# Even mixer of a two-block network: 8 of the 31 convolution taps as ScalarE copies added by GpSimd

## Chip, cores and metric

The kernel runs as one program on one core of a Trainium2 chip. The metric is the device time of one execution in microseconds (us); the time of the kernel before is the median of three runs. Engines are named as in the profile: PE is TensorE (PEld its weight loads), DVE is VectorE, ACT is ScalarE, POOL is GpSimd, SP is SyncE.

## What is computed

The whole network is two residual blocks of two layers each on 256 tokens of width 1024 in float32. Only one part is touched, the even mixer of the second block:

```python
def even_mixer(h, w_in, sc_conv_w, cf_conv_w, cf_conv_b, cf_ln_g, cf_ln_b, w_out):
    z = h @ w_in                                   # [256, 2560]
    sc_b, sc_c, sc_x, cf_a, cf_g = split(z)        # five parts of 512 channels
    y_sc = sc_b * causal_dwconv_2(sc_c * sc_x, sc_conv_w)       # 3 taps
    u = cf_a * jax.nn.sigmoid(cf_g)
    u = causal_dwconv_2(u, cf_conv_w) + cf_conv_b               # 31 taps
    u = jax.nn.silu(layernorm(u, cf_ln_g, cf_ln_b))
    return jnp.concatenate([y_sc, u], axis=-1) @ w_out
```

`causal_dwconv_2` is depthwise: output channel c at token t is the sum over k of w[k, c] times input channel c at token t - 30 + k.

## The kernel before

Activations stand transposed: 128 channels on the partitions, 256 tokens along the row. So the 512 channels of the convolution are four blocks of [128, 256], and the kernel works on them in two halves of two blocks (b = 0 and b = 2).

Weights come in chunks of 256 columns. `chunk` (L252) loads one into `st` by a DMA of SP and splits it in pieces of [128, 1024]: ACT rounds a piece to float32r (`whi`, L279) and DVE subtracts that from the original (`wlo`, L280). Three buffers each hold `whi` and `wlo`. A product of a piece is three matmuls per 128x128 tile (`mm3`, L285): L288 and L289 take `whi`, L290 takes `wlo`. A piece of a projection (`gather_T`) is 24 matmuls.

`even` (L1236) does this. `glu` makes `u` for two blocks from the chunks pa and pg, with 30 columns of zeros ahead of the tokens. The 31 taps are shared out. Taps 0 to 11 are `conv_pe` (L1269): ACT writes a diagonal matrix `dg` with the tap's weights (L1277), and PE multiplies it by the shifted `u` (L1278) and adds up in the PSUM tile `pcv`. Tap 30 with the bias is one ACT instruction per block that begins `cv` (L1288). Taps 12 to 29 are `conv_dve`: one DVE instruction per tap and block, cv = u * weight + cv (L1292). L1298 then adds `pcv` to `cv`. `short` (L1300) makes the gated three-tap convolution from the chunks pc, px and pb: t = pc * R * R, cx = px * t, three taps into `cs` (ACT L1312, DVE L1314), a GpSimd product cs * R (L1316), y = pb * cs (L1319), and its split into `yh`, `yl`. `norm` (L1325) needs all four blocks of `cv`: the mean over channels by ones on PE (`pmean`, L1329), the difference (L1332), squares on ACT, their sum on PE (`pvar`, L1340), a chain of small DVE instructions for 1/sqrt, its spread over the partitions (`prow`, `RL`), scale, tanh, and `yh`, `yl` of blocks 4 to 7 (L298, L299).

The output product `pr` has two passes of four chunks: the first over blocks 0 to 3 (the short convolution), the second over blocks 4 to 7 (the normed long one). The second pass ends in the residual and begins the next feed-forward.

Steps of these parts are woven when the program is written (L1364 to L1366), and then the tile framework's scheduler, which plays the program through with its own estimates, sets the order on each engine. Each engine runs its own queue strictly in that order and waits on semaphores where it needs another's result.

Of the kernel before, what the change touches and what calls it, by code (L numbers as in the profile page):

```python
# [27 lines left out]
def _runs(*spans):  # L28
    """Chunks of 256 columns of the spans."""
    return [[(c, c + 256)] for a, b in spans for c in range(a, b, 256)]  # L30
# [10 lines left out]
def _rows(chunks, *kts):  # L41
    """Each chunk's columns with the row tiles (first, count) cut after kts."""
    cuts = [(sum(kts[:i]), k) for i, k in enumerate(kts)]
    return [(c, cut) for c in chunks for cut in cuts]


# Each weight's chunks: their columns, and their row tiles of 128 as (first, count).
# [22 lines left out]
def _pack(w, chunks):  # L70
    """[L, K, N] as the chunks one after the other, each [128, row tiles, columns]."""
    layers, n = w.shape[0], w.shape[-1]
    w = w.reshape(layers, -1, 128, n)
    parts = []
    for l in range(layers):
        for pieces, (k0, kk) in chunks:
            v = np.concatenate([w[l, k0:k0 + kk, :, a:b] for a, b in pieces], axis=2)
            parts.append(v.transpose(1, 0, 2).reshape(-1))
    return np.concatenate(parts)


def _lay_out_params(inp):
    """The small parameters side by side as [128, n]: channels on partitions, or copied to all."""
    cols = []

    def chan(a):
        a = np.asarray(a).reshape(-1, 128)
        cols.append(a.T)

    def taps(a):  # L90
        k, c = a.shape
        cols.append(a.reshape(k, c // 128, 128).transpose(2, 1, 0).reshape(128, -1))

    def row(a):
        cols.append(np.broadcast_to(np.asarray(a).reshape(1, -1), (128, np.asarray(a).size)))

    def pad(a):
        c = np.zeros((128, 1), np.float32)
        c[:a.size, 0] = a
        cols.append(c)  # L100

    at = {}

    def put(name, f, a):
        at[name] = sum(c.shape[1] for c in cols)
        f(a)

    put("ffa_norm0", chan, inp["ffa_norm"][0])
    put("first", chan, inp["ffa_norm"][1])
    at["ffa_norm1"] = at["first"]  # L110
    for l in range(2):
        for nm in ("mix_norm", "ffb_norm", "mla_cq_norm", "mla_ckv_norm"):
            put(f"{nm}{l}", chan, inp[nm][l])
        for nm in ("mla_q_norm", "mla_k_norm"):
            put(f"{nm}{l}", pad, inp[nm][l])
            put(f"{nm}_rope{l}", row, inp[nm][l][64:96])
        for nm in ("moba_q_norm", "moba_k_norm", "gdn_a_log", "gdn_dt_bias"):
            put(f"{nm}{l}", row, inp[nm][l])
        put(f"gdn_conv{l}", taps, inp["gdn_conv"][l])
        put(f"gdn_out_norm{l}", chan, inp["gdn_out_norm"][l])  # L120
        put(f"mix2_norm{l}", chan, inp["mix_norm_g_2"][l])
        put(f"ffn_norm{l}", chan, inp["ffn_norm_g_2"][l])
        put(f"ffn_conv_w{l}", taps, inp["ffn_conv_w_2"][l])
        put(f"ffn_conv_b{l}", chan, inp["ffn_conv_b_2"][l])
    put("sc_conv", taps, inp["ev_sc_conv_w_2"][0])
    put("cf_conv", taps, inp["ev_cf_conv_w_2"][0])
    put("cf_b", chan, inp["ev_cf_conv_b_2"])
    put("ln_g", chan, inp["ev_cf_ln_g_2"])
    put("ln_b", chan, inp["ev_cf_ln_b_2"])
    put("lru_conv", taps, inp["od_lru_conv_w_2"][0])  # L130
    put("lru_conv_b", chan, inp["od_lru_conv_b_2"])
    put("lru_ba", chan, inp["od_lru_ba_2"])
    put("lru_bx", chan, inp["od_lru_bx_2"])
    put("lru_lam", chan, inp["od_lru_lam_2"])
    for nm in ("od_q_norm_g_2", "od_k_norm_g_2"):
        put(nm, chan, np.concatenate([inp[nm][0], inp[nm][0]]))
    return at, np.concatenate(cols, axis=1)


def _constants():  # L140
    """Tables that depend on shapes alone, side by side as [128, n]."""
# [34 lines left out]
def _all(gen):  # L176
    """Emits the rest of a part; returns what it returns."""
    while True:
        try:
            next(gen)  # L180
        except StopIteration as e:
            return e.value


def _mix(main, fill, ratio):
    """Emits a part with ratio steps of another after each of its own."""
    due = 0.0
    while True:
        try:
            next(main)  # L190
        except StopIteration as e:
            return e.value
        due += ratio
        while due >= 1:
            due -= 1
            next(fill, None)


def _weave(*gens):
    """Steps of several parts in turn."""  # L200
# [11 lines left out]
def _chain(*gens):  # L212
    """One part after the other; those not begun or not finished stay usable."""
# [5 lines left out]
class _Net:  # L219
# [32 lines left out]
    def chunk(self, name, i, between=None):  # L252
        """Chunk i of a weight, split exactly into two float32r parts: its pieces, each (first row
        tile, row tiles, high part, low part)."""
# [30 lines left out]
    def mm3(self, out, a, b, start, stop, **kw):  # L285
        """lhsT.T @ rhs of two split operands."""
# [14 lines left out]
    def rsqrt(self, v, n, name="rs"):  # L301
        """1/sqrt of a small tile of positive values."""
# [12 lines left out]
    def softplus(self, dst, x, n):  # L315
        """max(x, 0) + log1p(exp(-|x|)), the logarithm as 2 atanh(u / (2 + u))."""
# [16 lines left out]
    def rows(self, cols, name):  # L333
        """[128 tokens, 2] per-token values as a row over all partitions, [128, 256]."""
# [33 lines left out]
    def stats(self):  # L368
        """1/rms of the residual, per token as columns and as a row."""
# [15 lines left out]
    def gather_T(self, p, xs, pieces, first, last, col=0, blocks=2):  # L385
        """Adds the pieces' products to [128 features, blocks, 256 tokens] in one bank, in steps."""
# [8 lines left out]
    def gather_nat(self, p, xs, pieces, first, last, cols):  # L395
        """The same as [128 tokens, 2, cols]."""
# [21 lines left out]
    def residual(self, gain, name, layer, kts, xs, scale=None):  # L418
        """x += (a product in blocks of 128 features) [* R * scale], with the next norm's parts on
        the way; without a next norm, x goes out."""  # L420
# [130 lines left out]
    def heads(self, big, at, qk, v, sc, nsc):  # L551
        """Eight heads; qk(j) makes the transposed q and k of heads 2 j and 2 j + 1."""
# [27 lines left out]
    def rope(self, at, x, heads, d, tabs, t):  # L580
        """x [128, heads, d] in place; tabs hold gain * cos and gain * (sin, -sin)."""
# [106 lines left out]
    def gates(self, l, big, out, n, c):  # L688
        """Adds to out the tanh of half the branch's gate logits in half c of the channels."""
# [9 lines left out]
    def merge(self, l, big, mg, n, gate, br, last=None):  # L699
        """mg += 2 sigmoid(gate) * (branch @ w_branch)."""  # L700
# [191 lines left out]
    def gdn_gates(self, l, gp, csb):  # L892
        """beta and the decays: of each token from its chunk's start and to its end, of each chunk."""
# [32 lines left out]
    def gdn_decay(self, gp, scal):  # L926
        """[token, (tile, head), token of the chunk]: beta * decay, and the transposed decay."""
# [19 lines left out]
    def gdn_conv(self, l, big, wk, i):  # L947
        """2 silu(conv(.)) of the queries, keys or values, [128 dims, head, token]."""
# [20 lines left out]
    def gdn_keys(self, gk, at, raw, Dn):  # L969
        """The normalised keys and A, the strictly lower products that are to be inverted."""  # L970
# [40 lines left out]
    def inner(self, p, a, b):  # L1011
        """a.T @ b of each head's chunks, from [128 dims, (head, token)]."""
# [6 lines left out]
    def gdn_rest(self, out, wk, raw, scal, Dt, kn, knT):  # L1019
        """What the recurrence needs of the queries, the values and the keys."""  # L1020
# [46 lines left out]
    def gdn_invert(self, wk, A):  # L1067
        """Transposed inverses of I + A, by doubling the size of the inverted blocks."""
# [54 lines left out]
    def gdn_solve(self, out, us, M):  # L1123
        """u = (I + A)^-1 (v beta), and w = (I + A)^-1 (k beta exp(gcum)) transposed."""
# [19 lines left out]
    def gdn_scan(self, big, wk, scal, out, us, sz):  # L1144
        """The recurrence over the chunks, and the gated norm of what it gives."""
# [90 lines left out]
    def even(self, gain):  # L1236
        nc = self.nc
        v2 = lambda a: a.rearrange("p (b s) -> p b s", b=2)
        taps, on_pe = 31, 12
        with ExitStack() as ctx:  # L1240
# [12 lines left out]
            def glu(c):  # L1253
                """2 a sigmoid(g) of half c of the channels."""
# [14 lines left out]
            def conv_pe(b):  # L1269
                """Some of the taps of blocks b and b + 1 as products with diagonal matrices."""  # L1270
# [12 lines left out]

            def conv_dve(b):
# [5 lines left out]
                for k in range(on_pe, taps - 1):  # L1290
# [7 lines left out]
                nc.vector.tensor_tensor(cv[:, b:b + 2, :], cv[:, b:b + 2, :], v2(pcv[b]), op=OP.add)  # L1298

            def short(c):  # L1300
                """The gated short convolution of half c of the channels."""
# [23 lines left out]
            def norm():  # L1325
                """silu of the layer norm of the convolution."""
# [37 lines left out]
            fill = _chain(_weave(*(_chain(conv(0), conv(2)) for conv in (conv_pe, conv_dve))), norm())  # L1364
# [13 lines left out]
    def odd(self, gain):  # L1378
        nc = self.nc
        v2 = lambda a: a.rearrange("p (b s) -> p b s", b=2)  # L1380
        with ExitStack() as ctx:
# [43 lines left out]
            def qkv(i, z):  # L1425
                """The queries, keys or values; the first two normalised and transposed."""
# [135 lines left out]
    def lru_core(self, big, wk, xc, wa, wx, hs):  # L1562
        """The gated linear recurrence over the tokens."""
# [114 lines left out]
```

## Time and profile before

| | |
|---|---|
| time of three runs | 2027.24 us median, 2027.05 to 2028.5 |
| span of the profiled execution | 2022.9 us |
| PE busy over the span | 1997.5 us (99%) |
| DVE, ACT, POOL busy | 1450.4 us (72%), 1032.8 us (51%), 127.1 us (6%) |
| even mixer, from its first projection to its last | about 1402 to 1515 us after the start |

The span runs from the first to the last instruction of one execution; the device time of a run contains about 4.3 us more. Shares of the whole span are averages over stages with different limits, so the stage of the even mixer has to be read by itself. A busy PE is pipelined: a matmul of [128, 256] in float32r lasts 0.28 us in the record, but the next one starts 0.12 us after it, so a duration is not a price; the distance between two starts is. The same holds, less strongly, for DVE.

### The profile page before, as it was taken

Reading aid. Unit: us, or ns where it says so; the run is one execution under the profiler, and the core shown is the slowest. Engines: PE = TensorE matmul, PEld = TensorE weight load, DVE = VectorE, ACT = ScalarE, POOL = GpSimd, SP = SyncE. Lnnn points to the kernel's source line nnn. Section 1 sums busy time; section 2 is a strip of 40 time slices with the busy share of each in tenths; the row PEclk is TensorE's granted clock in tenths of the full one; section 3 lists DMA queues with packets and bytes.
Section 4 is the critical chain, followed back from the end, with each engine's and each line's share of the span. In section 5 each row is a group of like instructions: output and inputs, shape, how many; then the busy total and the mean of one; then the engine's idle time right before and its main releaser. Section 6 shows DMA issues by size and latency. Waiting matters only on the chain.

```text
span 2022.9 us, 40575 instructions
## 1 busy us (share of the span) xinstructions
PE 1997.5 (99%) x17004; PEld 1944.5 (96%) x17004; DVE 1450.4 (72%) x2585; ACT 1032.8 (51%) x1556; POOL 127.1 (6%) x158
## 2 busy tenths in 40 slices
PE   8999999999999999999999999999999999999999
PEld 8999998889999999999998999999999999989999
DVE  6665898747766676668987586666988866968874
ACT  5444665434544444446654454444655544656552
POOL 0000030220000000001203100000000000020000
PEclk9999999999999999999999999999999999999999
DMA  6455443224555555555432255555345555416554
GB/s 253 177 176 184 172 159 126 94 83 147 188 183 175 185 188 187 176 176 176 140 128 82 84 176 179 188 175 184 121 146 187 176 184 201 157 53 213 184 177 136
DMA packets 50711, 327.53 MB, mean 162 GB/s; under 512 B 6624, under 2 KB 8672, under 8 KB 18528
## 3 DMA queue, kind: packets, MB, share of 16 engines
q1 hardware_dynamic: 49296, 324.09, 45.8%
q8 instruction: 133, 2.18, 0.4%
q10 hardware_dynamic: 1232, 0.85, 0.2%
q14 instruction: 50, 0.41, 0.1%
HBM read 323.87 MB, written 1.05 MB: 161 GB/s over the span
## 4 chain that ended last, share of the span: by engine, by line
PE 95%; DVE 3%; issue 1%; ACT 1%; DMA 0%; POOL 0%; SPq 0%; DVEq 0%; ACTq 0%; POOLq 0%
PE pr L288 7%; PE pr L289 7%; PE pr L290 7%; PE pg L290 6%; PE pg L288 6%; PE pg L289 6%; PE pu L290 6%; PE pu L288 6%; PE pu L289 6%; PE pga L288 2%; PE pga L289 2%; PE pga L290 2%; PE pb L288 1%; PE pb L289 1%; PE pb L290 1%; PE pmq L288 1%
## 5 line engine op out<-in xcount | busy, mean ns | idle before, releaser
L279 ACT ACTIVATE whi<-st 128x1024 fp32r<-128x1024 f32 (+2 forms) x628 | 651.2, 1038 | 828.6 <-PE pr L289 201.6
L280 DVE TENSOR_TENSOR wlo<-st,whi 128x1024 fp32r<-128x1024 f32 (+2 forms) x628 | 756.9, 1206 | 383.7 <-ACT whi L279 378.7
L288 PE MATMUL pg<-xh,whi 128*128 128x256 f32 x1088 | 309.5, 284 | 9.3 <-ACT whi L279 9.3
L290 PE MATMUL pg<-xh,wlo 128*128 128x256 f32 x1088 | 309.1, 284 | 1.0 <-DVE wlo L280 1.0
L289 PE MATMUL pg<-xl,whi 128*128 128x256 f32 x1088 | 308.8, 284 | 0.0
L290 PE MATMUL pu<-xh,wlo 128*128 128x256 f32 x1056 | 299.6, 284 | 0.2 <-DVE wlo L280 0.2
L288 PE MATMUL pu<-xh,whi 128*128 128x256 f32 x1056 | 299.3, 283 | 0.0
L289 PE MATMUL pu<-xl,whi 128*128 128x256 f32 x1056 | 299.1, 283 | 0.0
L290 PE MATMUL pr<-gh,wlo 128*128 128x256 f32 x1056 | 297.4, 282 | 0.0
L289 PE MATMUL pr<-gl,whi 128*128 128x256 f32 x1056 | 297.4, 282 | 0.0
L288 PE MATMUL pr<-gh,whi 128*128 128x256 f32 x1056 | 297.4, 282 | 0.0
L288 PEld LDWEIGHTS pg<-xh,whi 128*128 128x128 f32 x1088 | 209.7, 193 | 9.3 <-ACT whi L279 9.3
L290 PEld LDWEIGHTS pg<-xh,wlo 128*128 128x128 f32 x1088 | 209.6, 193 | 1.5 <-DVE wlo L280 1.5
L289 PEld LDWEIGHTS pg<-xl,whi 128*128 128x128 f32 x1088 | 209.7, 193 | 0.0
L290 PEld LDWEIGHTS pu<-xh,wlo 128*128 128x128 f32 x1056 | 202.8, 192 | 0.4 <-DVE wlo L280 0.4
L288 PEld LDWEIGHTS pu<-xh,whi 128*128 128x128 f32 x1056 | 202.9, 192 | 0.0
L289 PEld LDWEIGHTS pu<-xl,whi 128*128 128x128 f32 x1056 | 202.9, 192 | 0.0
L288 PEld LDWEIGHTS pr<-gh,whi 128*128 128x128 f32 x1056 | 199.0, 188 | 0.0
L289 PEld LDWEIGHTS pr<-gl,whi 128*128 128x128 f32 x1056 | 199.0, 188 | 0.0
L290 PEld LDWEIGHTS pr<-gh,wlo 128*128 128x128 f32 x1056 | 198.9, 188 | 0.0
L288 PE MATMUL pga<-xh,whi 128*128 128x256 f32 x384 | 112.5, 293 | 0.0
L289 PE MATMUL pga<-xl,whi 128*128 128x256 f32 x384 | 109.3, 285 | 0.0
(548 smaller groups left out, 4029.6 us busy)
## 6 DMA issues: line engine op xcount, KB each, us to landing
st<-in_w_in_dram SPq DMA_DIRECT2D x52, 1024.0 KB, 4.8
st<-in_ffb_w_in_dram SPq DMA_DIRECT2D x44, 1024.0 KB, 4.9
st<-in_ffa_w_in_dram SPq DMA_DIRECT2D x43, 1024.0 KB, 4.8
st<-in_ffn_w_gate_dram SPq DMA_DIRECT2D x22, 1024.0 KB, 4.9
st<-in_ffn_w_up_dram SPq DMA_DIRECT2D x22, 1024.0 KB, 4.9
st<-in_ffa_w_out_dram SPq DMA_DIRECT2D x16, 896.0 KB, 4.5
st<-in_ffb_w_out_dram SPq DMA_DIRECT2D x16, 896.0 KB, 4.5
st<-in_ffn_w_down_dram SPq DMA_DIRECT2D x16, 896.0 KB, 4.5
```

Source lines behind the costliest of these rows:

```text
L279: self.hi = nc.scalar.activation(hi[:, :m], s, AF.Copy).ins
L280: nc.vector.tensor_tensor(lo[:, :m], s, hi[:, :m].bitcast(F32), op=OP.subtract)
L288: mm(out, a[0], b[0], start=start, stop=False, **kw)
L289: mm(out, a[0], b[1], start=False, stop=False, **kw)
L290: mm(out, a[1], b[0], start=False, stop=stop, **kw)
```

## The change

Docstrings and comments are gone, which moves line numbers by up to 15 and does nothing else. The core:

```diff
-        taps, on_pe = 31, 12
+        taps, on_pe, on_pool = 31, 6, 14
...
+            cp = big.tile([128, 4, S], F32, name="cp")
+
+            def conv_pool(b):
+
+                while b not in have:
+                    yield
+                for k in range(on_pe, on_pool):
+                    t = cp[:, b:b + 2, :] if k == on_pe else wk.tile([128, 2, S], F32, tag="ct", bufs=3, name="ct")
+                    for e in range(2):
+                        nc.scalar.activation(t[:, e, :], u[:, b + e, k:k + S], AF.Copy, scale=CW(b + e, k))
+                    if k > on_pe:
+                        nc.gpsimd.tensor_tensor(cp[:, b:b + 2, :], cp[:, b:b + 2, :], t, op=OP.add)
+                    yield
...
-                for k in range(on_pe, taps - 1):
+                for k in range(on_pool, taps - 1):
...
                 nc.vector.tensor_tensor(cv[:, b:b + 2, :], cv[:, b:b + 2, :], v2(pcv[b]), op=OP.add)
+                nc.vector.tensor_tensor(cv[:, b:b + 2, :], cv[:, b:b + 2, :], cp[:, b:b + 2, :], op=OP.add)
...
-            fill = _chain(_weave(*(_chain(conv(0), conv(2)) for conv in (conv_pe, conv_dve))), norm())
+            fill = _chain(_weave(*(_chain(conv(0), conv(2)) for conv in (conv_pe, conv_pool, conv_dve))), norm())
```

Taps 0 to 5 stay on PE, taps 14 to 29 on DVE. Taps 6 to 13 are new: for each tap and half ACT writes u * weight into `ct` (three buffers; the first tap straight into `cp`), and GpSimd adds `ct` to `cp`. At the end DVE adds `cp` to `cv`. Per half that is 16 ACT copies, 7 GpSimd adds of [128, 512] and one DVE add.

The scheduler's order moves with it. On GpSimd the adds come ahead of the two products cs * R of the short convolution (13 of 14 ahead of the first):

```order
-L1411 MEMSET lz 128x2x3 x2
 L1246 MEMSET u 128x4x30
-L1304 MEMSET cx 128x2x2 x2
-L1316 TENSOR_TENSOR cs<-cs,R 128x512 x2
+L1319 MEMSET cx 128x2x2 x2
+L1295 TENSOR_TENSOR cp<-cp,ct 128x512 x13
+L1331 TENSOR_TENSOR cs<-cs,R 128x512
+L1295 TENSOR_TENSOR cp<-cp,ct 128x512
+L1331 TENSOR_TENSOR cs<-cs,R 128x512
+L495 MEMSET z 128x2x2 x2
```

So where that queue held two products in this stage, it now holds sixteen operations of the same size. On DVE, the end of the convolution; first the kernel before, from the last long row of taps to the difference from the mean:

```order
L1292 SCALAR_TENSOR_TENSOR cv<-u,cw,cv 128x256 x9
L280 TENSOR_TENSOR wlo<-st,whi 128x1024
L1292 SCALAR_TENSOR_TENSOR cv<-u,cw,cv 128x256
L1298 TENSOR_TENSOR cv<-cv,pcv 128x512
L1292 SCALAR_TENSOR_TENSOR cv<-u,cw,cv 128x256 x3
L1308 TENSOR_TENSOR cx<-px,t_17690 128x2x256
L1292 SCALAR_TENSOR_TENSOR cv<-u,cw,cv 128x256
L280 TENSOR_TENSOR wlo<-st,whi 128x1024
L1298 TENSOR_TENSOR cv<-cv,pcv 128x512
L1314 SCALAR_TENSOR_TENSOR cs<-cx,P,cs 128x256 x4
L280 TENSOR_TENSOR wlo<-st,whi 128x1024
L1332 TENSOR_TENSOR cv<-cv,mean 128x1024
```

And the same place of the changed kernel:

```order
L1329 SCALAR_TENSOR_TENSOR cs<-cx,P,cs 128x256 x2
L1306 SCALAR_TENSOR_TENSOR cv<-u,cw,cv 128x256 x2
L280 TENSOR_TENSOR wlo<-st,whi 128x1024
L1329 SCALAR_TENSOR_TENSOR cs<-cx,P,cs 128x256 x2
L1306 SCALAR_TENSOR_TENSOR cv<-u,cw,cv 128x256 x5
L1334 TENSOR_TENSOR y<-pb,cs 128x512
L1306 SCALAR_TENSOR_TENSOR cv<-u,cw,cv 128x256 x3
L296 TENSOR_TENSOR yl<-y,yh 128x512
L1306 SCALAR_TENSOR_TENSOR cv<-u,cw,cv 128x256
L1312 TENSOR_TENSOR cv<-cv,pcv 128x512
L1313 TENSOR_TENSOR cv<-cv,cp 128x512
L280 TENSOR_TENSOR wlo<-st,whi 128x1024
```

The second half of the short convolution (cs, y, yl) stood behind the end of the long one and now stands ahead of it. On PE the second `pmean`, which waits for that end, stood among the matmuls of the chunk pb:

```order
L289 MATMUL pb<-xl,whi 128x256
L1329 MATMUL pmean<-cv,ones 128x256 x2
L290 MATMUL pb<-xh,wlo 128x256
L288 MATMUL pb<-xh,whi 128x256
L289 MATMUL pb<-xl,whi 128x256
```

In the changed kernel the same instruction stands in the first pass of the output product:

```order
L289 MATMUL pr<-yl,whi 128x256
L1344 MATMUL pmean<-cv,ones 128x256 x2
L290 MATMUL pr<-yh,wlo 128x256
L288 MATMUL pr<-yh,whi 128x256
L289 MATMUL pr<-yl,whi 128x256
```

Ahead of it 48 matmuls of that pass have to be done, and 46 more stand between it and `pvar`. In the odd mixer behind, a few matmuls of one attention head change places; nothing is added or taken away there.

## Rows read from the trace of the kernel before

**Rows 1.** Page, part 1: busy us, share of span, instructions.

```profile
PE 1997.5 (99%) x17004; PEld 1944.5 (96%) x17004; DVE 1450.4 (72%) x2585; ACT 1032.8 (51%) x1556; POOL 127.1 (6%) x158
```

**Rows 2.** Windows: length, busy PE, PEld, DVE, ACT, POOL, PEclk, DMA share, GB/s.

```profile
1428.50:1477.70 49.20, 49.20 (x335) 46.55 (x335) 47.64 (x96) 29.49 (x61) 3.04 (x1) 1.00 0.27 92
1477.70:1498.40 20.70, 18.73 (x154) 18.21 (x152) 17.36 (x36) 10.07 (x13) 1.30 (x1) 1.00 0.44 133
```

**Rows 3.** Tile pcv (durations ns, first and last start), and one step of the chain.

```profile
L1278 PE MATMUL pcv<-u,dg x96: 376/379/382, 1429.7 to 1474.5; 128*128 128x256 f32 x96
...
1437.88 0.43 PE pcv L1278 x2
```

**Rows 4.** Groups by line, 1428.5 to 1477.7: busy us, mean ns, idle before.

```profile
L1277 ACT ACTIVATE dg<-C,cw 128x128 f32<-128x128 f32 x44 | 17.2, 398 | 14.0 <-PE pcv L1278 13.5
...
L1312 ACT ACTIVATE cs<-cx,P 128x256 f32<-128x256 f32 x4 | 1.8, 498 | 0.2 <-DVE cx L1308 0.2
...
L1292 DVE SCALAR_TENSOR_TENSOR cv<-u,cw,cv 128x256 f32<-128x256 f32 x72 | 29.9, 471 | 0.0
L280 DVE TENSOR_TENSOR wlo<-st,whi 128x1024 fp32r<-128x1024 f32 x11 | 13.9, 1265 | 0.5 <-ACT whi L279 0.4
```

**Rows 5.** Timeline of DVE in the middle of the convolution: start, duration.

```profile
1444.19 0.67 DVE L1308 TENSOR_TENSOR cx<-px,t 128x512 f32<-128x512 f32 x1
1444.79 0.46 DVE L1292 SCALAR_TENSOR_TENSOR cv<-u,cw,cv 128x256 f32<-128x256 f32 x1
1445.18 1.21 DVE L280 TENSOR_TENSOR wlo<-st,whi 128x1024 fp32r<-128x1024 f32 x1
1446.32 1.66 DVE L1292 SCALAR_TENSOR_TENSOR cv<-u,cw,cv 128x256 f32<-128x256 f32 x4
```

**Rows 6.** Timeline of DVE and POOL around the first product cs * R.

```profile
1452.20 2.06 DVE L1292 SCALAR_TENSOR_TENSOR cv<-u,cw,cv 128x256 f32<-128x256 f32 x5
1452.36 3.04 POOL L1316 TENSOR_TENSOR cs<-cs,R 128x512 f32<-128x512 f32 x1 [47.74 <-DVE cs L1314]
1454.68 1.80 DVE L280 TENSOR_TENSOR wlo<-st,whi 128x1024 fp32r<-128x1024 f32 x1 [0.42 <-ACT whi L279]
```

**Rows 7.** Timelines of two other places where POOL and DVE overlap.

```profile
1479.48 1.30 POOL L1316 TENSOR_TENSOR cs<-cs,R 128x512 f32<-128x512 f32 x1 [24.07 <-DVE cs L1314]
1479.70 2.16 DVE L280 TENSOR_TENSOR wlo<-st,whi 128x1024 fp32r<-128x1024 f32 x1 [0.30 <-ACT whi L279]
...
276.67 1.53 POOL L586 TENSOR_TENSOR work<-mq,tqbcos 128x512 f32<-128x512 f32 x1 [19.43 <-DVE gy L962]
...
276.95 1.53 DVE L962 SCALAR_TENSOR_TENSOR gy<-gz,P,gy 128x256 f32<-128x256 f32 x1
```

**Rows 8.** Timelines from the convolution's end to the second output pass.

```profile
1477.14 0.68 DVE L1298 TENSOR_TENSOR cv<-cv,pcv 128x512 f32<-128x512 f32 x1
...
1480.56 1.03 PE L1329 MATMUL pmean<-cv,ones 128*128 128x256 f32 x4
...
1484.45 1.95 PE L1340 MATMUL pvar<-ones,sq 128*128 128x1 f32 x16 [0.36 <-ACT sq L1335]
...
1486.44 0.16 DVE L1343 TENSOR_SCALAR vln<-pvar 128x2 f32<-128x2 f32 x1 [0.79 <-PE pvar L1340]
...
1491.59 0.42 DVE L341 COPY RL<-prow 128x256 f32<-128x256 f32 x1
...
1498.38 0.62 PE L288 MATMUL pr<-yh,whi 128*128 128x256 f32 x3 [1.60 <-ACT yh L298]
...
1499.89 0.38 PE L289 MATMUL pr<-yl,whi 128*128 128x256 f32 x1 [0.89 <-DVE yl L299]
```

**Rows 9.** Timeline of PE at the program's start.

```profile
9.31 0.58 PE L288 MATMUL pg<-xh,whi 128*128 128x256 f32 x1 [9.31 <-ACT whi L279]
...
11.17 0.41 PE L289 MATMUL pg<-xl,whi 128*128 128x256 f32 x1
...
13.43 0.28 PE L288 MATMUL pg<-xh,whi 128*128 128x256 f32 x1
```

## The prediction

> **What bounds the kernel now.** I read the page's busy shares first. TensorE is busy 99% of the span [rows 1], which says that any matmul taken away shortens the program, but that is an average over 2023 us. So I read the stage next, in the view by windows [rows 2]. From 1428.5, where VectorE begins the taps, to 1477.7, where the convolution is closed, TensorE is busy 49.2 of 49.2 us and VectorE 47.6 of 49.2. Both are full; the reader is to see that the second number matters as much as the first. In the next window, from there to the first matmul of the second output pass, TensorE has lost 2 of 20.7 us: it waits for the layer norm's result, 1.60 us for `yh` and 0.89 us for `yl` [rows 8]. So the stage ends when VectorE's chain ends, and TensorE's matmuls only fill the time up to it. ScalarE has 29.5 of 49.2 us and GpSimd 3.0.
>
> **TensorE, taken away.** Each diagonal product is two records, one step of 0.43 us in the chain of work [rows 3]; 96 records are 48 products. 24 go: 24 x 0.43 = 10.3 us of TensorE's work between 1429 and 1475. This is the whole gain that can be had, and it counts only if VectorE comes free earlier too.
>
> **VectorE, the queue up to the close of the convolution.** Call the end of the last addition to `cv` the close. Prices are distances between starts [rows 5]: a tap 0.39 to 0.40 us (four in 1.66 us, the last 0.47 long), a weight split 1.14 (1445.18 to 1446.32), an operation of [128, 512] 0.60 (1444.19 to 1444.79). Before: 72 taps x 0.397 = 28.6 [rows 4], 10 splits x 1.14 = 11.4, 4 taps of `cs` 1.6, 9 operations of [128, 512] 5.4, together 47.0, and about 2 us of waits and of a stretched split; the close is at 1477.14 + 0.59 = 1477.7 [rows 8]. After: the order puts ahead of the close 64 taps (25.4), 13 splits (14.8), all 8 taps of `cs` (3.2), and 13 operations of [128, 512] (7.8), since `y`, `yl` and the two additions of `cp` now stand there: 51.2 us. ScalarE makes the first two copies ahead of `cv`'s start (two of 0.4 to 0.5 us, of which some 0.3 us are not covered), which delays the first tap. With no wait at all the close is at 1428.5 + 0.3 + 51.2 = 1480.0, **2.3 us later** than before. The 8 taps saved (3.2 us) are outweighed by work that the new order moved ahead.
>
> **GpSimd's adds, the disputed price.** 14 adds of [128, 512] are new, and both products cs * R now stand ahead of the close: 16 operations. One lasts 1.30 us where nothing held it up [rows 7], so GpSimd itself has room: 16 x 1.30 = 21 of 50 us. But the trace shows that the two engines take turns. At 1452.36 a GpSimd product begins while VectorE runs five taps; it takes 3.04 us and ends at 1455.40, which is 1.1 us after the last of the five taps, and the split that VectorE began at 1454.68 takes 1.80 instead of 1.21 [rows 6]. At 1479.48 the GpSimd product keeps its 1.30, and VectorE's split takes 2.16, 0.95 more [rows 7]. At 276.67 a GpSimd product waits for the end of one tap of another convolution, and the next tap, of the same form as ours, takes 1.53 instead of 0.47: 1.06 more [rows 4, 7]. In each case one engine stood still until the other had finished its instruction. The Trainium skill, page "SBUF — State Buffer", section "SBUF: two separate sides", states this as a rule that speaks against the change: a port pair that both engines use is locked for a whole instruction, by a GpSimd operation or by a VectorE one with two SBUF inputs, and the other blocks. By that rule alone the sum would take 16 x 1.30 = 20.8 us where the row of the tap gives 17.0; the trace agrees with it in kind.
>
> Taps, splits and `cs` have two inputs in SBUF; they are 43 of the 51 us. VectorE's queue there is full, so what stops it is not made up. Bounds: the smallest loss of the three rows, 0.59, gives 16 x 0.59 = 9.4 us; the whole length, 1.30, gives 20.8. I take the row that is nearest, a tap in a full queue: 16 x 1.06 = 17.0, and take off a tenth, an assumption, since `t`, `cx`, `y` and the additions of `pcv` read one input from PSUM (8 x 0.6 = 4.8 of 51 us) and may not compete: **15.3 us**. It does not matter who wins a turn: all 16 have to be done before the close, because VectorE waits there for `cp`, and `y` waits for cs * R behind the adds. The close is then at 1480.0 + 15.3 = 1495.3.
>
> **ScalarE.** 24 diagonals go (24 x 0.40 = 9.6 us) and 32 copies come (32 x 0.50 = 16 us; both [rows 4]): 29.5 + 6.4 = 36 us in a stretch that is now 66 long, so it hides. Queued behind the copies are the splits `whi`; a copy waits for one of three `ct` buffers, that is for the add three places ahead. The adds are ahead of that as long as GpSimd gets its turns, so I take 0, with up to 3 us in the range.
>
> **From the close to the second output pass.** Before, L289 of that pass starts at 1499.89, 22.2 us after the close [rows 8]. After, TensorE's order decides. `yl` of the short convolution ends 0.4 + 0.6 + 0.6 = 1.6 us ahead of the close (one tap, two additions). Then come 42 of the 48 matmuls ahead of the second `pmean`, at 0.12 each 5.0 (154 records in 18.73 us, [rows 2]), and 0.87 for the first `pmean`: the second starts 4.3 us after the close. It takes 0.87, and 46 more matmuls 5.5: `pvar` is at close + 10.7; its squares, 3.9 us after `pmean` as before (1480.56 to 1484.45), are there by 8.2. From `pvar` to `vln` 2.0, to `RL` 5.15 with one split in between as before, and from `RL` to L289 8.3 less the three splits that stand there no more, 8.3 - 3 x 1.14 = 4.9 [rows 8]. Sum 10.7 + 2.0 + 5.15 + 4.9 = 22.8, **0.6 us more** than before. So what TensorE saves ends as waiting: ahead of the first output pass and ahead of the second, each some 8 to 10 us.
>
> **TensorE's clock.** After standing idle for 9.31 us at the start, its matmuls last 0.41 us until about 13.3 and 0.28 from 13.43 on [rows 9]: some 4 us at half pace, which costs 2 us. The 1.60 us of idle time before 1498.38 were followed by no such stretch. The two new waits are as long as the first case: 0 to 2 x 2 us. The Trainium skill, "TensorE: Matmul & The Clock Gate", section "What's actually happening", says that the gate halves the clock of an array that stood idle; by it the upper end would hold. I take **2 us**, halfway, since the granted clock reads 1.00 (the upper level, 2.4 GHz) in both windows of [rows 2], with idle time in the second, and the start may be a case of its own.
>
> **Sum.** 2.3 + 15.3 + 0.6 + 2 = 20.2 us. On the profiled execution that is a span of 2022.9 + 20.2 = 2043; on the median 2027.24 + 20.2 = **2047 us**, 1% slower. Range of this case: 2027.2 + 2.3 + 9.4 + 0.6 = 2039.5 to 2027.2 + 2.3 + 20.8 + 0.6 + 4 + 3 = 2058. A measurement of this kernel can tell 0.2%, about 4 us, from no change.
>
> **Rivals.**
> *Adds covered.* The adds fall beside work that doesn't compete, or in gaps. For it: VectorE has gaps when it waits for `whi`, and one operation in ten reads PSUM. Against it: 97% busy before (47.6 of 49.2), and the three rows above. Price: L near 0 to 4 us, so 2027.2 + 2.3 + 0.6 + (0 to 4) = 2030 to 2034; taken as 2030.
> *TensorE decides, and the change is faster.* Place: the first output pass. If VectorE's queue reached the close early enough, the stage would shrink by the matmuls: 2027.2 - 10.3 = 2017. The second pass would then have to start at 1499.9 - 10.3 = 1489.6, so the close, 22.8 us ahead of that, at 1466.8: VectorE would have to do its 51.2 us of instructions in 38. For it stands only TensorE's 99%. Even a gain of 4 us needs 44.5.
> *ScalarE blocks the splits.* If the adds starve behind taps that follow one another (four taps passed GpSimd's product at 1452), copies wait for `ct`, and the `whi` behind them too, and TensorE and VectorE wait for those. The waits would come on top: with one tap row of nine (3.6 us) lost at each of three such places, 2047 + 11 = 2058, and more.
> *The change doesn't do what it says.* The order shows 24 products, 64 taps, 14 adds and 32 copies, so only the scheduler's shifts in the odd mixer are left, and they add no work: nearly excluded.
>
> **How the numbers follow.** Turns, as summed: 0.74. Adds covered: 0.11. TensorE decides: 0.04. ScalarE blocks: 0.10. Nothing of it: 0.01. The range leaves out the covered case (0.11), the faster ones (0.05) and the far end of the blocked one; from 2036, a little under the lower bound for a few adds in gaps, to 2058. Faster by over 0.2%: 0.05. Within 0.2%: most of the covered case, 0.08. Slower: 0.87.
>
> **What would show it.** In the profile after, taps (L1306) with a mean above 0.47 us, some of 1.4 to 1.6, and splits of 1.8 to 2.3 between 1428 and 1496; GpSimd adds that begin where the last ended and last 1.3 to 2.5; the difference from the mean some 20 us later than 1482; TensorE with idle time in front of `pr`, released by `yl` and `yh`, 10.3 us and more than the 2.5 before. Wrong: taps that stay at 0.47 while adds run (then the turns fall, and the time is near 2030), `whi` on ScalarE waiting for GpSimd (then the blocked case), or a close before 1480.

## The result: 0.85% slower, 2045.4 us where 2047 was predicted

| | before | after |
|---|---|---|
| median, us | 2027.83 (2027.05 to 2028.5, 4 runs) | 2045.36 (2044.58 to 2045.69, 4 runs) |
| span of the profiled execution, us | 2022.9 | 2043.8 |

The ratio is 1.0085, 95% interval 1.0073 to 1.0097: 17.5 us more by the medians, 20.9 by the two profiled spans. The working below accounts for the spans. In every execution with both figures on record the device time is 1.8 us above the span (2045.64 against 2043.8), not 4.3 as reckoned ahead of the prediction, so the profiled execution of the kernel before took about 2024.7 us, 3 less than its median (its runs beside the experiments go from 2024.8 to 2032.3), and that is the gap between the two figures.

The page of the changed kernel, part 1 (busy us, share of the span, instructions), answers to [rows 1].

```profile
PE 1998.2 (98%) x16956; PEld 1944.4 (95%) x16956; DVE 1463.3 (72%) x2579; ACT 1036.0 (51%) x1564; POOL 151.2 (7%) x172
```

TensorE has 48 matmul records fewer and is busy 0.7 us longer; GpSimd is busy 24 us longer for 14 instructions. The stage is seen in the view by windows, which answers to [rows 2] (length, busy PE, PEld, DVE, ACT, POOL with counts, granted clock, DMA share, GB/s): from the first tap to the close of the convolution, from there to the second output pass, and two stretches of TensorE at half pace.

```profile
1429.00:1496.04 67.04, 52.43 (x347) 48.84 (x346) 65.81 (x98) 35.36 (x72) 28.64 (x16) 0.90 0.28 91
1496.04:1517.50 21.46, 13.53 (x94) 12.93 (x93) 12.53 (x29) 7.55 (x10) 0.00 (x0) 0.74 0.45 147
...
1493.20:1499.80 6.60, 6.47 (x31) 6.17 (x32) 3.36 (x7) 1.06 (x1) 0.00 (x0) 0.55 0.00 0
...
1517.40:1523.10 5.70, 5.65 (x26) 5.64 (x27) 1.34 (x2) 0.63 (x1) 0.21 (x4) 0.50 0.00 0
```

The first window was 49.2 us long and is 67.0. VectorE fills it as before (65.8), TensorE no longer does (52.4 of 67.0), and GpSimd's busy time went from 3.0 to 28.6 us. What fills VectorE is in the groups by line (busy us, mean ns of one, idle time before them and who ended it), against [rows 4].

```profile
L1306 DVE SCALAR_TENSOR_TENSOR cv<-u,cw,cv 128x256 f32<-128x256 f32 x64 | 40.6, 683 | 0.0
L1295 POOL TENSOR_TENSOR cp<-cp,ct 128x512 f32<-128x512 f32 x14 | 22.7, 1619 | 35.0 <-ACT ct L1293 34.6
...
L1293 ACT ACTIVATE ct<-u,cw 128x256 f32<-128x256 f32 x28 | 12.2, 493 | 0.0
...
L1331 POOL TENSOR_TENSOR cs<-cs,R 128x512 f32<-128x512 f32 x2 | 6.0, 3006 | 23.0 <-DVE cs L1329 23.0
```

72 taps had a mean of 471 ns; 64 have 683. The change took 8 taps from VectorE, and yet the taps keep it busy 10.7 us longer (40.6 against 29.9). Where the time sits is plain in VectorE's timeline (start, duration), to be held against [rows 5] and [rows 6].

```profile
1429.02 6.75 DVE L1306 SCALAR_TENSOR_TENSOR cv<-u,cw,cv 128x256 f32<-128x256 f32 x9
1435.69 1.78 DVE L1264 SCALAR_TENSOR_TENSOR u<-z,ua 128x512 f32<-128x512 f32 x1
...
1452.76 2.06 DVE L1306 SCALAR_TENSOR_TENSOR cv<-u,cw,cv 128x256 f32<-128x256 f32 x5
...
1455.88 4.37 DVE L1306 SCALAR_TENSOR_TENSOR cv<-u,cw,cv 128x256 f32<-128x256 f32 x3
...
1491.82 0.69 DVE L1334 TENSOR_TENSOR y<-pb,cs 128x512 f32<-128x512 f32 x1 [1.16 <-POOL cs L1331]
...
1495.44 0.69 DVE L1313 TENSOR_TENSOR cv<-cv,cp 128x512 f32<-128x512 f32 x1
```

The last of these rows is the close, at 1495.44 + 0.60 = 1496.04.

And GpSimd's timeline of the same stretch:

```profile
1430.23 4.46 POOL L1295 TENSOR_TENSOR cp<-cp,ct 128x512 f32<-128x512 f32 x3 [25.09 <-ACT ct L1293]
1435.34 1.58 POOL L1295 TENSOR_TENSOR cp<-cp,ct 128x512 f32<-128x512 f32 x1 [0.65 <-ACT ct L1293]
...
1442.37 1.28 POOL L1295 TENSOR_TENSOR cp<-cp,ct 128x512 f32<-128x512 f32 x1 [0.22 <-ACT ct L1293]
...
1454.14 7.23 POOL L1295 TENSOR_TENSOR cp<-cp,ct 128x512 f32<-128x512 f32 x4 [5.30 <-ACT ct L1293]
```

Nine taps beside three adds take 6.75 us; without adds they take 3.64 (eight steps of 0.397 and a last one of 0.47, [rows 4, 5]). The difference is 3.11, three times 1.04. Five taps at 1452.76 take 2.06, which is undisturbed, though GpSimd's row of four begins at 1454.14; its first add let the last of them and the split behind them pass. Three taps at 1455.88, beside that group of four adds, take 4.37 instead of 1.26: again 3.11. The fourth stall of the group is the tap of `cs` behind them, 1.48 instead of 0.47.

### The profile page after: what moved, and what is told of

It reads as the page before. It is cut to its first block, busy times and chain, and to the rows that moved or that the text cites. A ratio compares the mean times of both kernels' runs of the same rounds, so it can differ in the third digit from the quotient of the medians.

```text
span 2043.8 us, 40507 instructions
## 1 busy us (share of the span) xinstructions
PE 1998.2 (98%) x16956; PEld 1944.4 (95%) x16956; DVE 1463.3 (72%) x2579; ACT 1036.0 (51%) x1564; POOL 151.2 (7%) x172
## 3 DMA queue, kind: packets, MB, share of 16 engines
HBM read 323.87 MB, written 1.05 MB: 159 GB/s over the span
## 4 chain that ended last, share of the span: by engine, by line
PE 92%; DVE 5%; issue 1%; ACT 1%; DMA 1%; POOL 0%; DVEq 0%; SPq 0%; ACTq 0%; POOLq 0%
PE pr L288 7%; PE pr L289 7%; PE pr L290 7%; PE pg L290 6%; PE pg L288 6%; PE pg L289 6%; PE pu L290 6%; PE pu L288 6%; PE pu L289 6%; PE pga L288 2%; PE pga L289 2%; PE pga L290 2%; DVE cv L1306 2%; DVE wlo L280 1%; PE pb L288 1%; PE pb L289 1%
## 5 line engine op out<-in xcount | busy, mean ns | idle before, releaser
L289 PE MATMUL pg<-xl,whi 128*128 128x256 f32 x1088 | 308.6, 284 | 0.0
L289 PE MATMUL pu<-xl,whi 128*128 128x256 f32 x1056 | 298.8, 283 | 0.0
L289 PE MATMUL pr<-gl,whi 128*128 128x256 f32 x1056 | 297.2, 281 | 0.0
L289 PEld LDWEIGHTS pg<-xl,whi 128*128 128x128 f32 x1088 | 209.7, 193 | 0.0
L289 PEld LDWEIGHTS pu<-xl,whi 128*128 128x128 f32 x1056 | 202.7, 192 | 0.0
L289 PEld LDWEIGHTS pr<-gl,whi 128*128 128x128 f32 x1056 | 198.8, 188 | 0.0
L289 PE MATMUL pga<-xl,whi 128*128 128x256 f32 x384 | 109.2, 284 | 0.0
```

The costliest lines, as they stand in the source:

```text
L289: mm(out, a[0], b[1], start=False, stop=False, **kw)
```

## The experiments

All times are medians; each ratio is to the kernel before on the same chip. The close is the end of the last addition to `cv`, as in the prediction. The theory was that VectorE's queue sets the close, that each GpSimd operation beside it stops it for about 1.04 us, and that TensorE's work is worth nothing while this holds. The rival was that TensorE's order, or the weaving of the code, makes the loss. The stage itself begins 0.5 to 1.4 us later in these profiled executions than in that of the kernel before, so distances within the stage say more than absolute times.

### Only TensorE's half of the change

```diff
-                    for k in range(on_pe):
+                    for k in range(6):
```

> The kernel before with 6 of the 12 diagonal products left out and nothing in their place (24 products, 10.3 us of TensorE; so part of the convolution is missing). Theory (VectorE's queue bounds the stage, TensorE only fills it): the order puts 72 taps, 12 splits, 8 taps of cs and 11 operations of [128, 512] ahead of the convolution's close, 28.6 + 13.7 + 3.2 + 6.6 = 52.1 us where 49.2 were, so no gain: 2028 to 2033 us. Rival (TensorE bounds the stage, what it is spared comes off): 2017 us.

Measured: 2031.04 us, ratio 1.0025 (1.0012 to 1.0037). 24 products, 10.3 us of TensorE's work, are gone, nothing takes their place, and the kernel is not faster. VectorE's timeline:

```profile
1480.07 0.69 DVE L1319 TENSOR_TENSOR y<-pb,cs 128x512 f32<-128x512 f32 x1 [0.57 <-POOL cs L1316]
...
1482.97 0.69 DVE L1298 TENSOR_TENSOR cv<-cv,pcv 128x512 f32<-128x512 f32 x1
```

TensorE's:

```profile
1479.55 2.07 PE L1329 MATMUL pmean<-cv,ones 128*128 128x256 f32 x4 [3.42 <-DVE cv L1298]
...
1504.00 1.01 PE L288 MATMUL pr<-yh,whi 128*128 128x256 f32 x3 [4.54 <-ACT yh L298]
```

The close moved from 1477.73 to 1483.6, later, not earlier; from the first tap it is 53.8 us away where it was 49.2. VectorE's taps are all there (72), but in the new order all 8 taps of `cs`, two more splits, `y` and `yl` stand ahead of the close: 52.0 us of instructions at the prices of the prediction instead of 47.0. TensorE spends what it saved waiting, 3.4 us for `cv`, 3.2 ahead of `prow` and 4.5 for `yh`. So this run has the queue's term without GpSimd's: with TensorE's shorter work the program's order hands VectorE the short convolution earlier.

### Only GpSimd's adds, and half of them

```diff
+            def idle_adds(b):
+                while b not in have:
+                    yield
+                for k in range(7):
+                    nc.gpsimd.tensor_tensor(sp, sp, u[:, b:b + 2, k:k + S], op=OP.add)
+                    yield
```

> The kernel before, all taps where they were, with 14 GpSimd adds of [128, 512] of shifted u into a scratch tile that nothing reads; VectorE's order stays that of the kernel before. Theory (a GpSimd add and a VectorE instruction with two SBUF inputs take turns, 1.04 us lost per add): VectorE's queue grows by 14 x 1.04 = 14.6 us, some of it in its 1.5 us of gaps: 2039 to 2044 us, with taps of about 1.5 us in the trace. Rival (the new order, the copies or the missing products made the changed kernel slow, the adds are covered): 2028 us.

> The kernel before, with 7 of the 14 idle GpSimd adds of the earlier run (4 while the first two channel blocks are at work, 3 in the second two). Theory: each add costs VectorE's queue one turn, so half the adds cost about half: the close 5 to 7 us later than before (14 adds: 11.8 us) and 2031 to 2036 us, part of it covered by slack behind the close. Rival: the first adds alone upset the balance, or it is GpSimd's being busy at all that slows VectorE; then the loss is near that of 14, 2038 to 2042, or near none.

With the second kernel only k = 0, 2, 4, 6 of the first two blocks and 1, 3, 5 of the others are added. VectorE's instructions up to the close are those of the kernel before, one by one. Measured: 14 adds 2041.4 us, ratio 1.0073 (1.0056 to 1.009); 7 adds 2034.93 us, 1.0038 (1.0023 to 1.0053). The taps in the groups by line, with 14 adds:

```profile
L1302 DVE SCALAR_TENSOR_TENSOR cv<-u,cw,cv 128x256 f32<-128x256 f32 x72 | 40.6, 618 | 0.0
```

With 7 adds:

```profile
L1302 DVE SCALAR_TENSOR_TENSOR cv<-u,cw,cv 128x256 f32<-128x256 f32 x72 | 34.7, 538 | 0.0
```

The close, with 7 adds and then with 14:

```profile
1483.19 0.68 DVE L1308 TENSOR_TENSOR cv<-cv,pcv 128x512 f32<-128x512 f32 x1
...
1489.57 0.67 DVE L1308 TENSOR_TENSOR cv<-cv,pcv 128x512 f32<-128x512 f32 x1
```

That is 1483.8 and 1490.2, where it was 1477.73 with no added work. Part of this is the later start: counted from the second instruction of L1262 ahead of the taps (1424.42, 1425.43 and 1425.86 in the three kernels), the close comes 5.1 and 11.0 us later. The rows of VectorE that are longer than unstalled add up to 6.4 and 12.3 us, so an add costs 0.9 us however many there are; 1.3 us of either sum were covered by waits that VectorE had before. The adds' results are read by nobody, so this is not data that somebody waits for. One row of VectorE's timeline with 14 adds shows the price at its clearest:

```profile
1439.66 6.75 DVE L1302 SCALAR_TENSOR_TENSOR cv<-u,cw,cv 128x256 f32<-128x256 f32 x5
```

Five taps that take 2.06 us alone take 6.75 here: 4.69 more, 0.94 for each of the five adds between them. Why it is 0.9 here and 1.04 in the changed kernel is open. The kernels lose more than their closes, 7.5 and 13.3 us by the medians. With 7 adds TensorE runs at half pace in the second output pass (granted clock 0.61 from 1505.8 to 1514.5), with 14 at a place far behind the mixer (0.57 from 1804 to 1816), so the price is read from the rows and not from these times.

### One input instead of two

The same fourteen instructions as copies, `nc.gpsimd.tensor_copy(sp, u[:, b:b + 2, k:k + S])`.

> The kernel before, with 14 GpSimd copies of [128, 512] (one input in SBUF, where an add has two) beside the taps, into a tile that nobody reads; VectorE's own order is as before. Theory: any GpSimd instruction on SBUF takes its turn with VectorE's taps, so the copies stop them as the adds did, by something between half an add's price (one input of two, 0.5 us) and the whole (1.04 us): 14 x 0.5 to 14 x 1.04 = 7 to 14.5 us on the close, 2033 to 2041 us, and taps with a mean well over 0.47. Rival: only an operation with two inputs in SBUF competes; taps stay at 0.47 and the time at 2027 to 2029.

Measured: 2030.16 us, ratio 1.0013 (1.0003 to 1.0022), under both bounds of the theory and a little over the rival's. The groups:

```profile
L1302 DVE SCALAR_TENSOR_TENSOR cv<-u,cw,cv 128x256 f32<-128x256 f32 x72 | 34.6, 535 | 0.0
...
L1291 POOL COPY sp<-u 128x512 f32<-128x512 f32 x14 | 11.4, 812 | 23.1 <-DVE u L1264 22.3
```

The taps took 4.7 us more (29.9 before), so copies compete as well. Of these, 1.0 is the price of the product cs * R, which fell on a split before, and `u` and two splits were held up beside the copies for another 0.9; all the rows that lengthened beside copies give 4.5 us, 0.32 for each, about a third of an idle add. The close came at 1481.6, 3.9 us later, 3.2 of them after the later start of the stage. The kernel lost 2.8. Why a copy costs a third and not a half is open.

### The change with adds of 8 columns

```diff
-                        nc.gpsimd.tensor_tensor(cp[:, b:b + 2, :], cp[:, b:b + 2, :], t, op=OP.add)
+                        nc.gpsimd.tensor_tensor(cp[:, b:b + 2, 0:8], cp[:, b:b + 2, 0:8], t[:, :, 0:8], op=OP.add)
```

> The changed kernel with the 14 GpSimd adds on 8 of the 256 columns only (the rest of the 8 taps is left out); copies, buffers and waits stay. Theory (the adds' length is the price): the close comes at 1428.8 + 25.4 + 13.7 + 3.2 + 7.8 = 1479, plus 1 to 3 us for two full products and 14 short adds: 2029 to 2034 us. Rival (ScalarE's copies, their three buffers and the order are the price): 2041 us or more.

Measured: 2026.76 us, ratio 0.9997 (0.9987 to 1.0006), 2 us under what was expected. ScalarE's 32 copies and the missing products are all there, and ahead of the close stand the same instructions, a few taps and splits in other places; only the adds' length is gone, and with it the loss: 1.0085 less 0.9997 is 17.8 us. So the change gains nothing even with adds that cost almost nothing. Its taps and adds, its first taps and its close:

```profile
L1306 DVE SCALAR_TENSOR_TENSOR cv<-u,cw,cv 128x256 f32<-128x256 f32 x64 | 29.1, 506 | 0.0
L1295 POOL TENSOR_TENSOR cp<-cp,ct 128x16 f32<-128x16 f32 x14 | 8.7, 623 | 39.5 <-ACT ct L1293 39.4
...
1429.44 3.64 DVE L1306 SCALAR_TENSOR_TENSOR cv<-u,cw,cv 128x256 f32<-128x256 f32 x9
...
1481.13 0.69 DVE L1313 TENSOR_TENSOR cv<-cv,cp 128x512 f32<-128x512 f32 x1
```

The close at 1481.7 is where it was expected; the 2 us lie behind it, where the second output pass begins 18.6 us after the close (21.4 in the changed kernel).

### The change with the adds on VectorE

The same line as `nc.vector.tensor_tensor` over all columns.

> The changed kernel with the 14 adds on VectorE instead of GpSimd (0.60 us each, 8.4 us in the full queue). Theory (an add on GpSimd costs VectorE 1.04 us, more than doing it itself): faster than the changed kernel by 14 x 0.44 = 6 us less what the order changes: 2037 to 2042 us. Rival (the adds on GpSimd cost VectorE little and another wait is the price): 8 us slower than the changed kernel, about 2054 us.

Measured: 2036.34 us, ratio 1.0046 (1.0031 to 1.0061), 0.7 us under the range that was expected.

```profile
L1306 DVE SCALAR_TENSOR_TENSOR cv<-u,cw,cv 128x256 f32<-128x256 f32 x64 | 27.5, 471 | 0.0
L1295 DVE TENSOR_TENSOR cp<-cp,ct 128x512 f32<-128x512 f32 x14 | 10.0, 711 | 0.0
...
1429.52 1.66 DVE L1306 SCALAR_TENSOR_TENSOR cv<-u,cw,cv 128x256 f32<-128x256 f32 x4
...
1489.27 0.69 DVE L1313 TENSOR_TENSOR cv<-cv,cp 128x512 f32<-128x512 f32 x1
```

The taps are back at 471 ns. VectorE does the fourteen adds itself in 10.0 us and the kernel is about 8 us faster than with GpSimd's help (1.0085 less 1.0046). ScalarE's copies, which both have, do not explain the loss. This gives the price once more without any list of stalls: from the first tap to the close are 52.3 us with adds of 8 columns, 60.4 with the adds on VectorE and 67.0 with the adds on GpSimd. That is 0.58 us for an add that VectorE makes itself and 1.05 for one that GpSimd makes.

### What TensorE and VectorE are worth, apart and together

VectorE's side is cut by `for k in range(18, taps - 1)` in place of `range(on_pe, taps - 1)`; the second kernel has that and the cut of the first experiment.

> The kernel before, with 6 of VectorE's 18 taps of each channel block left out and nothing in their place (the taps' share of the convolution is missing): 24 instructions x 0.397 = 9.5 us less on VectorE; TensorE keeps all 48 products. Theory: TensorE was full as well up to the close (49.2 of 49.2 us in the kernel before), so only its 2.5 us of waiting ahead of the second output pass can be had: 2025 to 2028 us. The close of the convolution comes near 1467 (the order puts 35.7 us of instructions ahead of it, with 2 us of waits), and that gains nothing by itself. Rival, VectorE alone is the bound: 2028 - 9.5 = 2018.

> The kernel before, with 6 of TensorE's 12 diagonal products and 6 of VectorE's 18 taps of each channel block left out, nothing in their place (half of TensorE's and a third of VectorE's part of the convolution is missing): 10.3 us less on TensorE and 9.5 us less on VectorE. Theory: the two engines were balanced, and only both cuts together shorten the stage: about 10 us, 2016 to 2021 us, where the cut on TensorE alone gave +0.25% and the cut on VectorE alone should give at most 2.5. Rival, something else sets the end of the stage (ScalarE's splits, the weights' transfers): within 4 us of the kernel before, 2024 to 2030.

Measured: 2026.29 us, ratio 0.9996 (0.9987 to 1.0006) with VectorE's cut; 2017.9 us, ratio 0.9953 (0.994 to 0.9967) with both. This gives a square: 10.3 us off TensorE alone +0.25%, 9.5 us off VectorE alone nothing, both together -9.5 us by the ratio. With VectorE's cut alone it is VectorE that waits, as the view by waits (waiter and tile, who ended it: us, times, longest) shows:

```profile
DVE t L1306 <- PE pc L290: 3.2, 1, 3.2
DVE cv L1298 <- PE pcv L1278: 2.5, 1, 2.5
```

So the close did not come near 1467, as expected, but at 1477.0, held by TensorE's products (1476.42, the end of the second wait) much where it stood before. The stage was balanced: either engine alone holds the close. The 2.5 us of waits ahead of the second output pass stayed (1.60 for `yh` and 0.95 for `yl`, much as in [rows 8]), so the lower end expected, 2025, was not reached.

### GpSimd's two old products on VectorE

> The kernel before, with GpSimd's two products cs * R done by VectorE instead. Theory: each such product on GpSimd stops VectorE for 1.04 us, and costs it 0.60 to do itself; the first stands in its full queue, the second near the close. 0.5 to 1.5 us faster than before, so 2026.5 to 2027.5, near or under what a measurement can tell. Rival, GpSimd's product is free beside VectorE: the queue grows by 2 x 0.6, 2029 to 2030.

Measured: 2032.51 us, ratio 1.0022 (1.0013 to 1.0031): slower by 4.7 us, where 1 us faster was expected. No row of the convolution is stalled any more, but the product itself and one more tap of `cs` stand ahead of the close and VectorE waits 0.9 us for `whi` at two places, so from the first tap (1429.62) to the close (1479.66) are 50.0 us, 49.2 before. The loss is behind the close, in TensorE's timeline:

```profile
1482.79 1.03 PE L1329 MATMUL pmean<-cv,ones 128*128 128x256 f32 x4
...
1487.39 0.39 PE L289 MATMUL pr<-yl,whi 128*128 128x256 f32 x1 [0.45 <-DVE yl L296]
1490.10 1.84 PE L1340 MATMUL pvar<-ones,sq 128*128 128x1 f32 x16
...
1504.52 1.01 PE L288 MATMUL pr<-yh,whi 128*128 128x256 f32 x3 [5.68 <-ACT yh L298]
```

Moving the products changed the order: VectorE now does cs * R, a split and `y` between the second `pmean` and the mean's subtraction, which begins at 1485.52 (1482.05 before), and on TensorE `pvar` stands behind matmuls of `pr` that wait for `yh` and `yl`. It comes 10.4 us behind the close, where it came 6.7 behind it. So this run does not tell what a product is worth on either engine; it tells that two moved instructions of 0.6 us can cost over 4 by the order that follows from them.

### Work for TensorE in the wait

```diff
+                pf = self.ps("pfill")
+                for k in range(5):
+                    nc.tensor.matmul(pf[:, :S], self.ones, u[:, 0, k:k + S], start=(k == 0), stop=(k == 4))
                 for b2 in range(2):
```

> The changed kernel, with five idle products of ones with u (128x256, 0.43 us each at full pace) on TensorE behind the row of 1/std (prow), where it waits 4.5 us for the second half of yh; they go to a PSUM tile that nobody reads. In the changed kernel the matmuls behind that wait last 0.41 instead of 0.28 us from 1517.45 to 1523, at 0.21 instead of 0.12 us apart: 26 steps x 0.09 = 2.3 us. Theory: the half pace follows the idle time; with TensorE at work in the wait most of it goes, 1 to 2.3 us faster than the changed kernel, ratio to before 1.0073 to 1.0081 instead of 1.0085, and granted clock near 1 where the second pass begins. Rival: the half pace comes from something else and stays; time as the changed kernel, or up to 1 us more if the products end after yh.

Measured: 2043.37 us, ratio 1.0078 (1.0062 to 1.0093), 2 us under the changed kernel by the medians and 1.4 by the ratios, whose intervals overlap, so the rows decide. TensorE's timeline:

```profile
1513.26 4.20 PE L1365 MATMUL pfill<-u,ones 128*128 128x256 f32 x10
1518.01 0.62 PE L288 MATMUL pr<-yh,whi 128*128 128x256 f32 x3 [0.55 <-ACT yh L298]
...
1519.07 0.28 PE L288 MATMUL pr<-yh,whi 128*128 128x256 f32 x1
```

The window of the second pass with the idle products:

```profile
1517.00:1525.00 8.00, 7.34 (x57) 6.69 (x57) 3.81 (x7) 3.35 (x7) 0.21 (x4) 1.00 0.00 1
```

The same window of the changed kernel:

```profile
1517.00:1525.00 8.00, 7.55 (x42) 7.54 (x43) 1.92 (x4) 1.30 (x3) 0.21 (x4) 0.62 0.00 0
```

The idle products themselves run at half pace; behind them the matmuls of the second pass last 0.28 instead of 0.41 us and the granted clock is 1.00 where it was 0.62 from 1517 to 1525 (1.00 is the level of 2.4 GHz, 0.50 that of 1.2). From the pass's first matmul to the first addition of the residual (L440) are 5.2 us here and 7.4 in the changed kernel. So the half pace in the second pass came from the idle time ahead of it, and cost about 2 us.

## Why the prediction was right, step by step

**GpSimd's turns, 15.3 us predicted: 16.8.** Every row of VectorE that exceeds its unstalled length was added up: 3.11 for the nine taps at 1429.02, 1.10 for `u`, and so on through 15 stalls of 1.01 to 1.10, 15.6 us, and 1.16 us that `y` waited for `cs`. That is 16 operations at 1.05, the price of the row taken from another convolution (1.06, [rows 7]). The tenth that was taken off for operations that read PSUM was wrong here: no GpSimd operation met such a row (so whether they compete is not shown), and none of the sixteen was free. Nor was a split held up, as the prediction had it; up to the close each lasted 1.20 to 1.22. The stalls fell on taps, on `u` and on one tap of `cs`. The bounds 9.4 and 20.8 stand on either side, and the rule of the Trainium skill, page "SBUF — State Buffer", section "SBUF: two separate sides", holds in kind: one engine stands while the other runs an instruction. By the adds' own unstalled length (1.28 at 1442.37) it would give 16 x 1.28 = 20.5 us, and the rows show 16.8.

**The queue to the close, 2.3: 1.0.** From the first tap to the close are 67.0 us; less 16.8 they are 50.2, against 49.2 before. The prediction had 51.2 and 0.3: it counted 13 splits, and 12 stand there; and VectorE had no idle time ahead of the first tap (which comes 0.5 us later, as does the whole stage). One premise was too strong: TensorE's matmuls do not only fill the time up to the close, since they held it at 1477.0 when VectorE alone was relieved.

**From the close to the second pass, +0.6: 0.0, by two errors that cancel.** From the close (1496.04) to L289 of the second pass (1518.25) are 22.2 us, as before. The prediction put 42 matmuls of `pr` and the first `pmean` behind the short convolution's `yl`; more of the 48 and that `pmean` had run already, and 31 stand between the wait for `yh` and the second `pmean`. But twenty of them ran at half pace, 0.21 us apart instead of 0.12, which cost 1.9 us. So it is luck that this term came out right. The chain from `pvar` to L289 was 12.1 us, summed to 12.05.

```profile
1493.22 1.01 PE L288 MATMUL pr<-yh,whi 128*128 128x256 f32 x3 [4.54 <-ACT yh L295]
...
1494.94 0.41 PE L288 MATMUL pr<-yh,whi 128*128 128x256 f32 x1
...
1499.80 1.03 PE L1344 MATMUL pmean<-cv,ones 128*128 128x256 f32 x4
...
1506.12 1.84 PE L1355 MATMUL pvar<-ones,sq 128*128 128x1 f32 x16
...
1517.45 1.01 PE L288 MATMUL pr<-yh,whi 128*128 128x256 f32 x3 [4.54 <-ACT yh L298]
1518.25 0.50 PE L289 MATMUL pr<-yl,whi 128*128 128x256 f32 x1
```

What TensorE saved did end as waiting, but not as placed. The prediction had 8 to 10 us ahead of each output pass; the rows show 4.54 ahead of each, 3.39 ahead of `prow`, and 10.0 for VectorE's splits, 2.1 of these in `pr` and the rest in the chunks (waiter and tile, who ended it: us, times, longest):

```profile
PE pc L290 <- DVE wlo L280: 2.8, 1, 2.8
PE pb L290 <- DVE wlo L280: 2.6, 1, 2.6
PE px L290 <- DVE wlo L280: 2.5, 1, 2.5
```

The sum does not hang on it, since VectorE's queue sets the close either way. A small misreading stands beside it: of the 2 us that TensorE lost in the second window of [rows 2], 0.36 were for the squares ahead of `pvar`; the 0.89 for `yl` lies behind that window.

**The clock, 2 us, halfway: 4.2.** Both waits that the prediction named were followed by half pace, 1.9 us lost in the first output pass and 26 steps x 0.09 = 2.3 us in the second, the upper end of its range. The 1.9 are already in the 0.0 above. So the case that was read from the program's start ([rows 9]) is no case of its own. The Trainium skill, "TensorE: Matmul & The Clock Gate", section "What's actually happening", agrees with both rows: an array that stood idle came back at the lower level.

**ScalarE, 0: it hid.** 35.4 us of 67.0, and the one wait that VectorE had in the first window is that for `cs`.

Together: 0.5 us by which the stage already began later, 17.8 to the close (16.8 + 1.0), 0.0, and 2.3 in the second pass are 20.6 of the 20.9 us. By the medians it is 17.5. The mechanism was right, VectorE's full queue stopped at every GpSimd operation. That the sum, 20.2, lies so near is partly luck: the turns were 1.5 too low and the clock 2.2 too low, the queue 1.3 too high and the way from the close, counted without its 1.9 us of half pace, 2.5 too high.

**The rivals.** Adds covered would have been 2030: one add let the end of a row of taps and a split pass (1454.14), and then took its turn as every other did. TensorE deciding would have been 2017: that needs VectorE's cut as well. ScalarE blocking the splits did not happen.

## What to carry to other kernels

Before moving element-wise work to an idle GpSimd, ask whether VectorE's queue is full where it would run: here each 512-column add that GpSimd took cost VectorE 1.04 us (0.9 in the kernels with idle adds), and about 0.6 if VectorE made it itself. Where two engines are both full up to the same point, taking work from one gives nothing (+0.25% and 0.0% here, -9.5 us for both at once), so price a change by the engine that stays full. And read the order that follows from the change: counted from the first tap, it moved the close by 1 to 4.5 us in kernels where no price had changed.

## What the runs showed that was not expected

- The granted clock shows the lower level here, which in the profiled execution of the kernel before it never did while matmuls ran, not even at the program's start where those of [rows 9] lasted 0.41 us (so a 1.00 there does not speak against half pace): 0.55 and 0.50 behind the two waits of 4.5 us. It was also 0.52 from 1441.0 to 1444.5 and 0.51 from 1465.0 to 1468.4, behind waits of 2.5 and 2.8 us for `wlo`, while a wait of 2.6 us at 1452.89 was followed by none; how long a wait was does not settle it.
- In the kernel with narrow adds, TensorE waited 2.34 us for `yh` at 1477.32, ran on at full pace, and went to half pace only at 1479.6, for 3.4 us: the lower level can begin 2.3 us behind the wait, in the middle of work. The window:

```profile
1479.60:1483.00 3.40, 3.40 (x18) 3.40 (x17) 2.68 (x5) 1.06 (x1) 0.00 (x0) 0.50 0.00 0
```

- A GpSimd copy of [128, 512] cost VectorE 0.32 us where an idle add cost 0.9.
- Who gets a turn is not settled by order of arrival alone: mostly an add came in at the next boundary between two taps, but the one at 1454.14, both products of the changed kernel (2.98 and 3.03 us long) and the one at 1452.36 in the kernel before stood through several of VectorE's instructions.
